# Expert weights as 2 MiB transfers into ten pair places, with the SBUF pools laid out anew

## The chip, the cores and the metric

The kernel is one program on 1 core of a Trainium2 chip. Its metric is the device time of one execution in microseconds (us), and the time of a kernel is the median of several executions. Beside the times there is one profiled execution with its trace: engines PE (TensorE), DVE (VectorE), ACT (ScalarE), POOL (GpSimd) and SP (SyncE, which here only issues transfers).

## What is computed

Two transformer blocks on 256 tokens of width 1024, all in float32. What matters here is how much weight each part reads:

```python
# first block: mixing (short convolution, gated delta rule, attention), then
u = causal_dwconv(h @ w_ffn_up[l], w_ffn_conv[l])
x = x + (jax.nn.silu(gate) * val) @ w_ffn_down[l]
# second block: modulation, two attentions, then 32 experts, four for each token
mod = jax.nn.silu(c) @ w_ada[l] + b_ada[l]
proj = h @ w_in[l]
...
hh = xb @ w1[e] + b1[e]
return swiglu_clamped(hh) @ w2[e] + b2[e]
```

Every expert has 8 MiB of `w1` and 4 MiB of `w2`, so 32 experts read 384 MiB. The dense weights of both blocks are 91 MiB.

## The kernel before

**Slabs.** All weights are packed on the host into slabs of 1 MiB: 128 partitions with 2048 float32 each, a row of 8 KB to a partition. `ws_in` holds the dense slabs in the order of their use, `we_in` twelve slabs for each expert (eight of `w1`, four of `w2`). One transfer on SP's queue brings one slab.

**Dense part.** A pool "A" of six places (`NA = 6`) takes the dense slabs. `load_slabs` (L192) issues the load of slab n once slab n-6 has been read in the program's order (L196), and `slab_read` (L251) calls it. There are two kinds of dense slab. The kind "s" is split by ACT and DVE or POOL into two float32r parts (`split`, L381; the hi part is L388, the lo part L393), two units to a slab, four units ahead of the products that use them. The kind "a" (`ada`, L475) is read by PE directly, at L483, and eight of them make one third of the modulation. The list `WS` mixes the two kinds: three "a" slabs ahead of the 15th "s" slab, five ahead of the 21st, one each ahead of the 39th, 42nd, 45th and 48th, and eight more inside the second block's attention. PE reads an "a" slab later than ACT and DVE split the "s" slabs behind it, since splitting runs ahead. Which of the six places a load gets is decided by the pool (L199): it takes one that has been given back.

**Expert part.** `load_m` (L215) loads the slabs of the experts in the order of `ORDER`. Places stand in the string `TURNS`, one letter for each of 19 slabs, named for the pool that holds it: X, A, B, C, D, E and O. They come free one after another as the dense part ends, and are then filled (`load_all`, L235). When PE has read a slab, `free_m` (L240) loads the next into the same place, but for the place "O", which is given back; so 18 places go round. `first_rounds` (L1693) and `second` (L1731, L1736) are the expert's products; an expert has a capacity of 32 to 128 tokens (`CAPS`), in pieces of 64 and 32, and its slabs are freed in its last piece.

**Queue.** All these transfers stand in SP's queue in the order of the program, and SP waits for one before it issues the next. A transfer also waits for the eighth before it, since eight semaphores go round.

```python
            if n >= NA and n - NA not in read:
                break
            if n < len(WS):
                t = slabs.tile([P, SW], F32, name="w")
```

Of the kernel before, what the change touches and what calls it, by code (L numbers as in the profile page):

```python
# [10 lines left out]
F32 = mybir.dt.float32  # L11
# [10 lines left out]
P = 128  # L22
T = 256
# [8 lines left out]
BIG = 3.0e38  # L32
NA = 6

TURNS = "XAAABBDODAAACCCCEEE"
NS = len(TURNS)
# [125 lines left out]
def kernel(ctx: ExitStack, tc: tile.TileContext, x_in, cols_in, rows_in, const_in, cona_in, conb_in, rpb_in,  # L162
# [4 lines left out]
    small = ctx.enter_context(tc.tile_pool(name="small", bufs=2))  # L167
    pools = {k: ctx.enter_context(tc.tile_pool(name="slabs" + k, bufs=TURNS.count(k))) for k in "ABCE"}
    slabs = pools["A"]
# [20 lines left out]
    read = set()  # L190

    def load_slabs(upto=10 ** 6):  # L192

        while state["loaded"] < min(upto, len(WS) + NA):
            n = state["loaded"]
            if n >= NA and n - NA not in read:  # L196
                break
            if n < len(WS):
                t = slabs.tile([P, SW], F32, name="w")  # L199
                for h in range(1 if n else 2):  # L200
                    o = slice(0, SW) if n else slice(h * UW, (h + 1) * UW)
                    nc.sync.dma_start(t[:, o], ws_in[n, :, o])
                s_slab[n] = t
            else:
                load_m([m for m in range(NS) if TURNS[m] == "A"][n - len(WS)])
            state["loaded"] += 1
# [8 lines left out]
    def load_m(m, pool=None):  # L215

        pos, i = divmod(m, 12)
        if pos >= len(ORDER):
            return
        rank = ORDER[pos]  # L220
        i = ((0, 2, 4, 6, 1, 3, 5, 7) if CAPS[rank] == 32 else (0, 2, 1, 3, 4, 6, 5, 7))[i] if i < 8 else i
# [142 lines left out]

    so = ctx.enter_context(ExitStack())


    with sx:
# [41 lines left out]

        hTh = pools["B"].tile([P, KC, T], F32R, name="hTh", tag="w")
        hTl = pools["B"].tile([P, KC, T], F32R, name="hTl", tag="w")
        yTh = pools["E"].tile([P, KC, T], F32R, name="yTh", tag="w")
        yTl = pools["E"].tile([P, KC, T], F32R, name="yTl", tag="w")
        xn = pools["E"].tile([P, 2, D], F32, name="xn", tag="w")

# [549 lines left out]
        with ExitStack() as s2:  # L966
# [40 lines left out]
            with ExitStack() as s3:  # L1007
# [77 lines left out]
                def add_norms(c):  # L1085
# [12 lines left out]
                    for h in range(2):  # L1098
# [9 lines left out]

            pools["X"] = ctx.enter_context(tc.tile_pool(name="slabsX", bufs=TURNS.count("X"), side="right",
                                                        reuse_waits="tile"))  # L1110
            s4 = sx.enter_context(ExitStack())
# [6 lines left out]
            load_all("X")  # L1118
            with ExitStack() as s3:
# [30 lines left out]
            with ExitStack() as s3:  # L1150
# [207 lines left out]
                def projections2():  # L1358
# [15 lines left out]
                    for kc in range(KC - LAST):  # L1374
                        while count["joined"] <= kc:
                            yield 0, 0.1
                        if "D" not in pools and (count["turned"] == 8 or kc == KC - LAST - 1):
                            while count["turned"] < 8:
                                yield 0, 0.1
                            s4.close()  # L1380
                            for n in "DO":
                                pools[n] = (ctx if n == "D" else so).enter_context(
                                    tc.tile_pool(name="slabs" + n, bufs=TURNS.count(n), side="right", reuse_waits="tile"))
                            load_all("DO")
# [109 lines left out]

    load_all("CE")
    s6 = ctx.enter_context(ExitStack())
# [185 lines left out]
    def first_rounds(w, blk, w1, onehot, free=None):  # L1682
# [33 lines left out]
    def second(w, blk, acts, w2, free=None):  # L1716
# [9 lines left out]
        for bi, bl in enumerate(BO):  # L1726
# [52 lines left out]
    def spare(name):  # L1779

        t = [m_pool[m] for m in range(12 * NE - NS + 1, 12 * NE - 12) if m_pool[m] in "BD"][len(spares)]
        spares.append(pools[t].tile([P, SW], F32, name=name, tag="w"))
        return spares[-1]
# [11 lines left out]
    for pos, rank in enumerate(ORDER):  # L1795
        m0_ = 12 * pos
        w1 = lambda bl, i: m_slab[m0_ + 2 * BO.index(bl) + i].rearrange("p (k n) -> p k n", k=4)
        free = lambda ks: free_m([m0_ + k for k in ks])
        w2 = lambda bi: m_slab[m0_ + 8 + bi].rearrange("p (k n) -> p k n", k=2)
        nxt = None  # L1800
# [32 lines left out]
        if pos == 0:  # L1833
            so.close()
            ek2 = ctx.enter_context(tc.tile_pool(name="ek2", bufs=2, side="right", reuse_waits="tile"))
            for _ in que:
# [28 lines left out]

    fs = [spare("fs") for _ in range(2)]
    fr = late.tile([P, 2], F32, name="fr")
# [41 lines left out]
    with tc.For_i(0, n_over, 1):  # L1909
        with ExitStack() as s7:  # L1910
# [6 lines left out]

            def load(i):
                t = slabs.tile([P, SW], F32, name="w")
                nc.sync.dma_start(t, we_in[ds(reg, 1), i].rearrange("a p n -> p (a n)"))  # L1920
                return t

            for n in range(4):
# [5 lines left out]
                def w1(bl, i):  # L1929
                    if (bl, i) not in w1t:  # L1930
                        w1t[bl, i] = load(2 * BO.index(bl) + i).rearrange("p (k n) -> p k n", k=4)
# [5 lines left out]
                w2t = [load(8 + i).rearrange("p (k n) -> p k n", k=2) for i in range(4)]  # L1937
                combine(blk, second(w, blk, a, lambda bi: w2t[bi]), into_acc)
# [33 lines left out]
def pack(inp):  # L1972
# [38 lines left out]
    w1, wd = f("w1_2")[0], f("w2_2")[0]  # L2011
    we = np.empty((NE, 12, P, SW), np.float32)
    a = w1.reshape(NE, KC, P, 4, 256, 2).transpose(0, 3, 2, 1, 5, 4)
    a = a.reshape(NE, 4, P, 2, 4 * 512).transpose(0, 1, 3, 2, 4)
    b = wd.reshape(NE, 4, 2, P, D).transpose(0, 1, 3, 2, 4).reshape(NE, 4, P, 2 * D)
    for i, bl in enumerate(BO):
        we[:, 2 * i:2 * i + 2] = a[:, bl]
        we[:, 8 + i] = b[:, bl]
    b1 = f("b1_2")[0].reshape(NE, 4, 256, 2).transpose(0, 1, 3, 2).reshape(NE, 2048)
# [47 lines left out]
```

## Time and profile before

| | us |
|---|---|
| median of 3 runs | 1521.78 (1520.45 to 1521.88) |
| the profiled execution, own time | 1518.86 |
| its span, first to last instruction | 1517.1 |
| PE busy | 1384.4 (91%) |
| DVE, ACT, POOL busy | 556.9, 449.1, 91.8 |

The profiled execution took 2.92 us less than the median. Up to about 555 us the program is the dense part, from 559 us to 1500 us the experts, and the last 17 us are the final norm and the output.

### The profile page before, as it was taken

To read this page: it belongs to the slowest core of one execution; us is meant where nothing else is said; L and a number is where in the kernel's file an instruction comes from. 1 tells how busy PE (TensorE), PEld (TensorE's weight loads), DVE (VectorE), ACT (ScalarE), POOL (GpSimd) and SP (SyncE) were. 2 spreads that over 40 slices of the span, in tenths; PEclk is the share of its full clock that TensorE was granted. 3 is DMA by queue.
4 is the path that set the end of the run, shared out by engine and by line. 5 is a ranking of instruction groups with operands and counts; after the bars stand their busy time and mean duration, and the time that the engine had idled before them with its cause. 6 is when DMAs were issued, how large, how long until landed. Compare 5 with 4: busy or idle time off the path is not lost.

```text
span 1517.1 us, 22468 instructions
## 1 busy us (share of the span) xinstructions
PE 1384.4 (91%) x8859; PEld 738.7 (49%) x8863; DVE 556.9 (37%) x1234; ACT 449.1 (30%) x975; POOL 91.8 (6%) x42
## 2 busy tenths in 40 slices
PE   6999979999999999999999999999999987988774
PEld 6898779998668753333333333333333322222111
DVE  4854687776767741222212122221121101111102
ACT  6554545555646641111111111111121101101111
POOL 3322150000310000000000000000000000000000
PEclk9999999999999999999999999999999999999887
DMA  7322575666666489999999999999999999999994
GB/s 309 123 101 85 223 278 212 263 220 227 203 255 245 167 359 357 419 421 421 377 421 386 388 414 416 421 421 420 420 421 421 420 421 420 421 421 420 421 421 183
DMA packets 71087, 506.72 MB, mean 334 GB/s; under 512 B 8096, under 2 KB 8352, under 8 KB 9952
## 3 DMA queue, kind: packets, MB, share of 16 engines
q1 hardware_dynamic: 70112, 503.50, 82.4%
q10 hardware_dynamic: 864, 1.72, 0.3%
q8 instruction: 72, 1.18, 0.3%
q14 instruction: 39, 0.32, 0.1%
HBM read 504.14 MB, written 1.05 MB: 333 GB/s over the span
## 4 chain that ended last, share of the span: by engine, by line
PE 61%; DMA 29%; DVE 5%; ACT 3%; issue 1%; SPq 0%; POOL 0%; ACTq 0%; DVEq 0%; POOLq 0%
DMA w<-in_we 28%; PE mm L1693 17%; PE mm L433 14%; PE mm L1736 6%; PE acc L1759 3%; PE acc L467 2%; PE acc L468 2%; PE acc L469 2%; PE mm L1651 2%; PE mm L1731 2%; DVE u L393 2%; DMA w<-in_ws 1%; PE mm L810 1%; PE mm L483 1%; PE mm L1662 1%
## 5 line engine op out<-in xcount | busy, mean ns | idle before, releaser
L1693 PE MATMUL mm<-w,xT 128*64 128x512 f32 (+1 forms) x2432 | 464.8, 633 | 56.8 <-DMA w<-in_we 56.5
L1693 PEld LDWEIGHTS mm<-w,xT 128*64 128x64 f32 (+1 forms) x2432 | 136.9, 130 | 366.8 <-issue 260.5
L1702 DVE TENSOR_SCALAR h<-mm 128x256 f32<-128x256 f32 x58 | 24.6, 425 | 728.2 <-PE mm L1698 728.2
L433 PE MATMUL mm<-hTh,u 128*128 128x256 f32 x1376 | 263.4, 289 | 8.8 <-DVE fcv L1043 7.2
L433 PEld LDWEIGHTS mm<-hTh,u 128*128 128x128 f32 x1376 | 220.4, 194 | 18.5 <-issue 14.3
L433 PE MATMUL mm<-hTl,u 128*128 128x256 f32 x688 | 196.3, 285 | 0.8 <-DVE hTl L422 0.8
L393 DVE TENSOR_TENSOR u<-w,u 128x1024 fp32r<-128x1024 f32 x115 | 160.8, 1403 | 68.0 <-ACT u L388 67.9
L1703 ACT ACTIVATE a<-h 128x256 f32<-128x256 f32 x58 | 24.2, 417 | 521.5 <-DVE h L1702 521.5
L388 ACT ACTIVATE u<-w 128x1024 fp32r<-128x1024 f32 x134 | 140.1, 1056 | 40.3 <-PE acc L469 30.0
L1736 PE MATMUL mm<-w,aT 128*64 128x512 f32 x640 | 141.7, 595 | 5.5 <-ACT aT L1714 5.4
L433 PEld LDWEIGHTS mm<-hTl,u 128*128 128x128 f32 x688 | 133.4, 194 | 2.0 <-DVE hTl L422 1.0
L1736 PEld LDWEIGHTS mm<-w,aT 128*64 128x64 f32 x640 | 44.1, 137 | 90.2 <-issue 79.1
L1741 ACT ACTIVATE y<-mm 128x512 f32<-128x512 f32 x38 | 22.7, 597 | 207.4 <-PE mm L1736 138.5
L1731 PE MATMUL mm<-w,aT 128*32 128x512 f32 x576 | 65.7, 595 | 9.9 <-ACT aT L1714 9.9
L1895 POOL TENSOR_TENSOR fs<-fs,x 128x512 f32<-128x512 f32 x1 | 1.3, 1261 | 960.6 <-ACT fr L300 960.6
L1651 PE MATMUL mm<-x,S 128*32 128x256 f32 (+1 forms) x448 | 56.7, 460 | 2.5 <-DVE S L1638 2.5
L393 POOL TENSOR_TENSOR u<-w,u 128x1024 fp32r<-128x1024 f32 x19 | 46.9, 2469 | 134.7 <-ACT u L388 134.7
L1043 DVE SCALAR_TENSOR_TENSOR fcv<-mm,cols,fcv 128x255 f32<-128x255 f32 x88 | 42.4, 482 | 26.6 <-ACT fcv L1040 25.1
L1669 ACT ACTIVATE xT<-mm,mod,gs 128x64 f32<-128x64 f32 (+1 forms) x152 | 46.6, 386 | 2.1 <-PE mm L1662 1.5
L1671 DVE TENSOR_SCALAR xT<-mm,gs,mod 128x64 f32<-128x64 f32 (+1 forms) x152 | 38.7, 320 | 3.0 <-PE mm L1662 3.0
L1731 PEld LDWEIGHTS mm<-w,aT 128*32 128x32 f32 x576 | 16.7, 109 | 46.8 <-issue 30.6
L1651 PEld LDWEIGHTS mm<-x,S 128*32 128x32 f32 (+1 forms) x448 | 18.6, 119 | 39.6 <-issue 28.3
(555 smaller groups left out, 1461.9 us busy)
## 6 DMA issues: line engine op xcount, KB each, us to landing
w<-in_we SPq DMA_DIRECT2D x384, 1024.0 KB, 19.8
w<-in_ws SPq DMA_DIRECT2D x90, 1024.0 KB, 5.0
nb<-in_rpb SPq DMA_DIRECT2D x4, 512.0 KB, 7.6
x<-in_x SPq DMA_DIRECT2D x2, 512.0 KB, 6.1
w<-in_ws SPq DMA_DIRECT2D x2, 512.0 KB, 7.6
bt<-in_b SPq DMA_DIRECT2D x3, 256.0 KB, 8.3
out<-fs SPq DMA_DIRECT2D x3, 256.0 KB, 3.1
grow<-in_wf ACTq DMA_DIRECT2D x1, 512.0 KB, 3.9
```

The costliest lines, as they stand in the source:

```text
L388: nc.scalar.activation(hi, raw, AF.Copy)
L393: eng.tensor_tensor(lo, raw, hi, op=OP.subtract)
L433: nc.tensor.matmul(b[:, 0:T], w[:, k, :], h[:, k, :], start=(n == 0), stop=(n == 3 * KC - 1))
L467: nc.tensor.matmul(o, th[:, kc, t], wh[:, w], start=first, stop=False)
L1043: nc.vector.scalar_tensor_tensor(t[:, sh:], b[:, :T - sh], w(2 - sh), t[:, sh:], op0=OP.mult, op1=OP.add)
L1651: nc.tensor.matmul(b[p * tb:(p + 1) * tb, 0:n], S[:, c, p * tb:(p + 1) * tb], x[:, c, p * n:(p + 1) * n], start=(c == 0), stop=(c == 1))
L1669: nc.scalar.activation(dst, src, AF.Identity, scale=gs[:, kc:kc + 1], bias=mod[:, 24 + kc:25 + kc])
L1671: nc.vector.tensor_scalar(dst, src, gs[:, kc:kc + 1], mod[:, 24 + kc:25 + kc], op0=OP.mult, op1=OP.add)
L1693: nc.tensor.matmul(b[p * tb:(p + 1) * tb, :], xT[:, k, q * tb:(q + 1) * tb], w1(p * nr + rd, kc // 4)[:, kc % 4, :], start=(kc == 0), stop ...
L1731: nc.tensor.matmul(b[p * tb:(p + 1) * tb, :], aT[:, 0, j, p0 * tb:(p0 + 1) * tb], w2(bi)[:, j, h * 512:(h + 1) * 512], start=(bi == 0), st ...
L1736: nc.tensor.matmul(b[p * tb:(p + 1) * tb, :], aT[:, rd, j, p0 * tb:(p0 + 1) * tb], w2(bi)[:, j, p * 512:(p + 1) * 512], start=(bi == 0 and ...
L1759: nc.tensor.matmul(acc[c][h], lhsT, rhs, start=False, stop=False, skip_group_check=True)
```

## The change

The experts' slabs are packed in pairs, two slabs side by side in one row: a transfer has 128 rows of 16 KB, 2 MiB. Ten places of 2 MiB stand in the new `TURNS`; all of them go round, so there are 20 MiB in place of 18 (19 at the start). The two slabs of a pair are those that are used together: two blocks of `w1` columns for the same half of the depth, or two neighbours of `w2`. A pair is freed when both are read.

The three pairs of pool A also take the dense slabs, slab by slab. They are no longer given out by the pool: slab n goes to half (n - N0) mod 6 of the three tiles `w_pair`, with N0 = len(WS) - 6 = 81. The rule for when a load is put into the program is the same as before. An expert's pair in A is loaded when both dense slabs of its halves are read.

The split parts `u` and the tile `xn` get pools of their own (`parts`, `xnp`), whose space the pools "C" and "G" take over after the dense part. `hTh` and `hTl` are halves of one tile, and so are `yTh` and `yTl`. The place "F" exists from the start.

```diff
-NA = 6
-TURNS = "XAAABBDODAAACCCCEEE"
+PW = 2 * SW
+NA = 3
+TURNS = "FABADACCEG"
...
+    w_pair = [slabs.tile([P, PW], F32, name="w") for _ in range(NA)]
+    N0 = len(WS) - 2 * NA
...
-            if n >= NA and n - NA not in read:
+            j = n - len(WS)
+            if n >= 2 * NA and not ({N0 + 2 * j, N0 + 2 * j + 1} if j >= 0 else {n - 2 * NA}) <= read:
                 break
-            if n < len(WS):
-                t = slabs.tile([P, SW], F32, name="w")
+            if j < 0:
+                i = (n - N0) % (2 * NA)
+                t = w_pair[i // 2][:, i % 2 * SW:(i % 2 + 1) * SW]
...
-        pos, i = divmod(m, 12)
+        pos, i = divmod(m, 6)
...
-        t = pools[m_pool[m]].tile([P, SW], F32, name="w")
+        t = pools[m_pool[m]].tile([P, PW], F32, name="w")
         nc.sync.dma_start(t, src)
...
         while state["freed"] in m_freed:
-            if m_pool[state["freed"]] != "O":
-                load_m(state["next"], m_pool[state["freed"]])
-                state["next"] += 1
+            load_m(state["next"], m_pool[state["freed"]])
+            state["next"] += 1
             state["freed"] += 1
...
-            t = pools["C"].tile([P, 2, UW], F32R, name="u", tag="w")
+            t = parts.tile([P, 2, UW], F32R, name="u")
...
-                    free([2 * BO.index(p * nr + rd) + kc // 4 for p in range(R)])
+                    free([j + kc // 4 for j in ((0, 2) if R == 4 else (2 * rd,))])
...
-            if free:
-                free([8 + bi])
+            if free and bi % 2:
+                free([4 + bi // 2])
```

**Order.** PE, DVE, ACT and POOL have the same compute instructions in the same order in both programs. What moves is on SP's queue. The first place is the end of the first block's mixing, where the first third of the modulation is computed. `w` are the tiles that a load fills, with the buffer's number; behind it stand the semaphores for which the load waits. Those named DMAHW are of earlier transfers, PE, DVE and Pool of the readers of what lay there. Before:

```order
L202 DMA w_1729<-in_ws 128x2048 [waits DMAHW1_49,DVE_49,Pool_49]
L202 DMA w_1735<-in_ws 128x2048 [waits DMAHW6_49,PE_49]
L202 DMA w_1924<-in_ws 128x2048 [waits DMAHW7_49,PE_49]
L202 DMA w_1926<-in_ws 128x2048 [waits DMAHW2_49,DMAHW0_49,DVE_49]
L202 DMA w_1928<-in_ws 128x2048 [waits DMAHW3_49,DVE_49]
L202 DMA w_1930<-in_ws 128x2048 [waits DMAHW4_49,DVE_49]
L202 DMA w_1932<-in_ws 128x2048 [waits PE_49]
L202 DMA w_1978<-in_ws 128x2048 [waits DMAHW0_49,PE_49]
```

The same eight slabs after the change, w_95 to w_97 being the three pairs:

```order
L211 DMA w_97<-in_ws 128x2048 [waits DMAHW6_49,PE_49]
L211 DMA w_95<-in_ws 128x2048 [waits DMAHW7_49,PE_49]
L211 DMA w_95<-in_ws 128x2048 [waits DMAHW0_49,PE_49]
L211 DMA w_96<-in_ws 128x2048 [waits DMAHW1_49,DVE_49,Pool_49]
L211 DMA w_96<-in_ws 128x2048 [waits DMAHW2_49,DVE_49]
L211 DMA w_97<-in_ws 128x2048 [waits DMAHW3_49,DVE_49]
L211 DMA w_97<-in_ws 128x2048 [waits DMAHW4_49,DVE_49]
L211 DMA w_95<-in_ws 128x2048 [waits DMAHW5_49,Pool_49]
```

They are the slabs 20 to 27 of `WS` (counted from 0). Before, the first three waits were for a split and two "a" slabs, and the third "a" slab came up at the seventh; now the three "a" slabs (14, 15 and 16) are waited for by the first three loads, and the other five stand behind them.

The second place is the first block's feed-forward, at the 39th "s" slab. Before:

```order
L202 DMA w_3412<-in_ws 128x2048 [waits DMAHW6_49,DMAHW4_49,DVE_49]
L202 DMA w_3414<-in_ws 128x2048 [waits DMAHW7_49,DMAHW5_49,DVE_49]
L202 DMA w_3416<-in_ws 128x2048 [waits DMAHW0_49,DVE_49]
L202 DMA w_3418<-in_ws 128x2048 [waits DMAHW3_49,DVE_49]
L202 DMA w_3594<-in_ws 128x2048 [waits PE_49]
```

And after the change:

```order
L211 DMA w_95<-in_ws 128x2048 [waits DMAHW4_49,PE_49]
L211 DMA w_96<-in_ws 128x2048 [waits DMAHW6_49,DMAHW5_49,DVE_49]
L211 DMA w_96<-in_ws 128x2048 [waits DMAHW7_49,DVE_49]
L211 DMA w_97<-in_ws 128x2048 [waits DMAHW0_49,DVE_49]
L211 DMA w_97<-in_ws 128x2048 [waits DMAHW2_49,PE_49]
```

The wait for PE's reading of the "a" slab stood at the fifth of these loads and stands at the first now; the same comes again at the next two "a" slabs.

## Rows read from the trace of the kernel before

**Rows 1.** The page's second part: 40 equal slices of the span, transfers.

```profile
DMA  7322575666666489999999999999999999999994
GB/s 309 123 101 85 223 278 212 263 220 227 203 255 245 167 359 357 419 421 421 377 421 386 388 414 416 421 421 420 420 421 421 420 421 420 421 421 420 421 421 183
```

**Rows 2.** The page's fourth part: shares of the chain that ended last.

```profile
PE 61%; DMA 29%; DVE 5%; ACT 3%; issue 1%; SPq 0%; POOL 0%; ACTq 0%; DVEq 0%; POOLq 0%
```

**Rows 3.** Windows of the experts: busy PE, PEld, DVE, ACT, POOL; PE clock, DMA share, GB/s.

```profile
600.00:720.00 120.00, 115.78 (x634) 41.17 (x632) 28.14 (x96) 19.50 (x53) 0.00 (x0) 1.00 1.01 420
...
830.00:850.00 20.00, 19.61 (x130) 6.58 (x128) 1.18 (x3) 3.17 (x8) 0.00 (x0) 1.00 0.78 298
...
950.00:1495.00 545.00, 474.66 (x2758) 152.80 (x2756) 90.73 (x290) 77.35 (x211) 0.00 (x0) 0.95 1.01 419
```

**Rows 4.** The chain in order of time, at 1045 us (start, us, what).

```profile
1045.55 19.76 DMA w<-in_we
```

**Rows 5.** Windows of the start: 4 KB rows alone, then 8 KB rows alone.

```profile
9.70:11.00 1.30, 1.30 (x7) 1.30 (x8) 0.62 (x6) 0.68 (x4) 0.00 (x0) 1.00 1.01 413
12.20:13.50 1.30, 1.30 (x7) 1.08 (x6) 1.30 (x6) 1.30 (x4) 0.00 (x0) 1.00 1.03 429
```

**Rows 6.** SP's timeline: two issues of expert slabs around 835 us.

```profile
834.62 0.33 SPq L231 DMA_DIRECT2D w<-in_we  x1
836.34 0.33 SPq L231 DMA_DIRECT2D w<-in_we  x1
```

**Rows 7.** The page's sixth part: dense loads, KB of one, median us to landing.

```profile
w<-in_ws SPq DMA_DIRECT2D x90, 1024.0 KB, 5.0
```

**Rows 8.** SP's timeline, the dense slabs 22, 23, 26 and 28.

```profile
160.34 0.33 SPq L202 DMA_DIRECT2D w<-in_ws  x1
167.28 0.33 SPq L202 DMA_DIRECT2D w<-in_ws  x1
184.20 0.33 SPq L202 DMA_DIRECT2D w<-in_ws  x1
186.94 0.40 SPq L202 DMA_DIRECT2D w<-in_ws  x1
```

**Rows 9.** PE's timeline from 182 us (start, us, instruction, count).

```profile
183.08 3.64 PE L483 MATMUL mm<-w,silc 128*32 128x512 f32 x32
186.65 1.09 PE L339 MATMUL mm<-cst,xn 128*128 128x128 f32 x8
```

**Rows 10.** ACT's and DVE's timelines from 187 us.

```profile
187.34 2.17 ACT L420 ACTIVATE hTh<-mm,cols 128x128 fp32r<-128x128 f32 x8
189.35 3.00 ACT L388 ACTIVATE u<-w 128x1024 fp32r<-128x1024 f32 x3
198.91 1.06 ACT L388 ACTIVATE u<-w 128x1024 fp32r<-128x1024 f32 x1 [5.22 <-DMA w<-in_ws]
191.44 3.72 DVE L393 TENSOR_TENSOR u<-w,u 128x1024 fp32r<-128x1024 f32 x2 [0.76 <-ACT u L388]
```

**Rows 11.** A window while the transfers of `bt` (32 partitions) run.

```profile
191.00:193.00 2.00, 2.00 (x19) 2.00 (x18) 1.56 (x1) 1.35 (x2) 1.93 (x1) 1.00 1.08 238
```

**Rows 12.** The feed-forward: issue of the slab of the 43rd "s", its split, PE, and the chain.

```profile
314.19 0.33 SPq L202 DMA_DIRECT2D w<-in_ws  x1
330.91 1.06 ACT L388 ACTIVATE u<-w 128x1024 fp32r<-128x1024 f32 x1 [0.32 <-PE acc L469]
333.61 1.06 PE L483 MATMUL mm<-w,silc 128*32 128x512 f32 x8
334.68 11.71 PE mm L433 x96
```

**Rows 13.** DVE's and PE's timelines in the second block's attention.

```profile
426.91 1.21 DVE L393 TENSOR_TENSOR u<-w,u 128x1024 fp32r<-128x1024 f32 x1
432.89 1.06 PE L483 MATMUL acc<-w,silc 128*32 128x512 f32 x8
```

**Rows 14.** Waits between 400 and 480 us (waiter, releaser, us, times, longest).

```profile
ACT u L388 <- DMA w<-in_ws: 3.8, 2, 2.0
```

More of the change, by code (lines that the diff above doesn't have):

```diff
@@ L167 @@
     small = ctx.enter_context(tc.tile_pool(name="small", bufs=2))
-    pools = {k: ctx.enter_context(tc.tile_pool(name="slabs" + k, bufs=TURNS.count(k))) for k in "ABCE"}
+    pools = {k: ctx.enter_context(tc.tile_pool(name="slabs" + k, bufs=TURNS.count(k))) for k in "ABEF"}
     slabs = pools["A"]
@@ L178 @@
     sx = ctx.enter_context(ExitStack())
+    parts = sx.enter_context(tc.tile_pool(name="parts", bufs=4))
+    xnp = sx.enter_context(tc.tile_pool(name="xnp", bufs=1))
     hp = sx.enter_context(tc.tile_pool(name="hp", bufs=1))
@@ L204, in load_slabs @@
             else:
-                load_m([m for m in range(NS) if TURNS[m] == "A"][n - len(WS)])
+                load_m([m for m in range(NS) if TURNS[m] == "A"][j])
             state["loaded"] += 1
@@ L409, in split_ahead @@
                 state["split"] += 1
[L411 to L415, printed above, removed]
+        hT2 = pools["B"].tile([P, 2, KC, T], F32R, name="hT2", tag="w")
+        yT2 = pools["E"].tile([P, 2, KC, T], F32R, name="yT2", tag="w")
+        hTh, hTl, yTh, yTl = hT2[:, 0], hT2[:, 1], yT2[:, 0], yT2[:, 1]
+        xn = xnp.tile([P, 2, D], F32, name="xn")
         def take_scaled(scale):
@@ L1106 @@
                 last_products(4, lambda i, cs, wh, wl: down(NFF - 4 + i, cs, wh, wl), add_norms, False)
-            pools["X"] = ctx.enter_context(tc.tile_pool(name="slabsX", bufs=TURNS.count("X"), side="right",
-                                                        reuse_waits="tile"))
             s4 = sx.enter_context(ExitStack())
@@ L1380, in projections2 @@
                             s4.close()
[L1381 to L1384, printed above, removed]
+                            pools["D"] = ctx.enter_context(tc.tile_pool(name="slabsD", bufs=1, side="right",
+                                                                        reuse_waits="tile"))
+                            load_all("D")
                         wh, wl = unit()
@@ L1467 @@
             keep_warm(WARM[5])
+    for k in "CG":
+        pools[k] = ctx.enter_context(tc.tile_pool(name="slabs" + k, bufs=TURNS.count(k), reuse_waits="tile"))
+    ek2 = ctx.enter_context(tc.tile_pool(name="ek2", bufs=2, side="right", reuse_waits="tile"))
     psa = ctx.enter_context(tc.tile_pool(name="psm", bufs=1, space=PSUM, reuse_waits="tile"))
@@ L1493, in open_work @@
         return w
-    load_all("CE")
+    load_all("CEG")
     s6 = ctx.enter_context(ExitStack())
@@ L1779, in spare @@
     def spare(name):
-        t = [m_pool[m] for m in range(12 * NE - NS + 1, 12 * NE - 12) if m_pool[m] in "BD"][len(spares)]
-        spares.append(pools[t].tile([P, SW], F32, name=name, tag="w"))
+        t = [m_pool[m] for m in range(6 * NE - NS, 6 * NE - 6) if m_pool[m] in "BD"][len(spares)]
+        spares.append(pools[t].tile([P, PW], F32, name=name, tag="w"))
         return spares[-1]
@@ L1795 @@
     for pos, rank in enumerate(ORDER):
-        m0_ = 12 * pos
-        w1 = lambda bl, i: m_slab[m0_ + 2 * BO.index(bl) + i].rearrange("p (k n) -> p k n", k=4)
+        m0_ = 6 * pos
+        of_pair = lambda j, i: m_slab[m0_ + j][:, i * SW:(i + 1) * SW]
+        w1 = lambda bl, i: of_pair(BO.index(bl) // 2 * 2 + i, BO.index(bl) % 2).rearrange("p (k n) -> p k n", k=4)
         free = lambda ks: free_m([m0_ + k for k in ks])
-        w2 = lambda bi: m_slab[m0_ + 8 + bi].rearrange("p (k n) -> p k n", k=2)
+        w2 = lambda bi: of_pair(4 + bi // 2, bi % 2).rearrange("p (k n) -> p k n", k=2)
         nxt = None
@@ L1833 @@
         if pos == 0:
-            so.close()
-            ek2 = ctx.enter_context(tc.tile_pool(name="ek2", bufs=2, side="right", reuse_waits="tile"))
             for _ in que:
@@ L1864 @@
     s6.close()
-    fs = [spare("fs") for _ in range(2)]
+    fs_ = spare("fs")
+    fs = [fs_[:, c * D:(c + 1) * D] for c in range(2)]
     fr = late.tile([P, 2], F32, name="fr")
@@ L1916, with load @@
                 nc.vector.tensor_scalar(oc[:, i:i + 1], ocap[:, 0:1], 64.0 * i, None, op0=OP.add)
-            def load(i):
+            def load(j, i):
                 t = slabs.tile([P, SW], F32, name="w")
-                nc.sync.dma_start(t, we_in[ds(reg, 1), i].rearrange("a p n -> p (a n)"))
+                nc.sync.dma_start(t, we_in[ds(reg, 1), j, :, i * SW:(i + 1) * SW].rearrange("a p n -> p (a n)"))
                 return t
@@ L1930, in w1 @@
                     if (bl, i) not in w1t:
-                        w1t[bl, i] = load(2 * BO.index(bl) + i).rearrange("p (k n) -> p k n", k=4)
+                        n_ = BO.index(bl)
+                        w1t[bl, i] = load(n_ // 2 * 2 + i, n_ % 2).rearrange("p (k n) -> p k n", k=4)
                     return w1t[bl, i]
@@ L1936 @@
                     pass
-                w2t = [load(8 + i).rearrange("p (k n) -> p k n", k=2) for i in range(4)]
+                w2t = [load(4 + i // 2, i % 2).rearrange("p (k n) -> p k n", k=2) for i in range(4)]
                 combine(blk, second(w, blk, a, lambda bi: w2t[bi]), into_acc)
@@ L2016, in pack @@
     for i, bl in enumerate(BO):
-        we[:, 2 * i:2 * i + 2] = a[:, bl]
-        we[:, 8 + i] = b[:, bl]
+        for h in range(2):
+            we[:, i // 2 * 2 + h, :, i % 2] = a[:, bl, h]
+        we[:, 4 + i // 2, :, i % 2] = b[:, bl]
+    we = we.reshape(NE, 6, P, PW)
     b1 = f("b1_2")[0].reshape(NE, 4, 256, 2).transpose(0, 1, 3, 2).reshape(NE, 2048)
```

14 lines of the change are left out of this document (6 added, 8 removed).

## The prediction

> **What bounds the kernel now.** I read the slices first. From 606 us on, the transfers move 419 to 421 GB/s in nearly every slice, with dips to 377 and 386; before, in the dense part, they move 85 to 359 [rows 1]. So bytes can bound the experts, not the dense part. The shares of the chain say the same in another way: PE 61%, DMA 29% [rows 2]. The windows tell where the bound changes: between 600 and 720 us PE is busy in 115.78 of 120 us while the transfers already run at full share; between 830 and 850 us the transfers' share falls to 0.78, because places are not free; from 950 to 1495 us PE is busy in 474.66 of 545 us and the transfers move 419 GB/s without a hole [rows 3]. The chain's DMA piece at 1045 us gives the price of a MiB: eight transfers are in flight together, and 19.76 us [rows 4] are eight of them, 2.47 us each (2.49 at 421 GB/s).
>
> From this two things follow. What the experts' transfers gain after the last wait for a place, at about 850 us, is gained at the end. And what the dense part loses is lost at the end too, unless the transfers can run on meanwhile; they can't, since the places are full when PE is late.
>
> **What doesn't change.** The arithmetic on PE, DVE, ACT and POOL, in order and size; the bytes (384 MiB for the experts); the issues on SP, 0.33 us each [rows 6], which have 2.5 us apiece: 192 fewer cost and give nothing.
>
> **Gain 1: one more pair goes round.** 18 MiB go round now, 20 then, so the transfers may be 2 MiB further ahead of PE at the last wait for a place: 2 × 2.49 = 5.0 us. But a pair is free only when both slabs are read, and the two places at 835 us came free at 834.62 and 836.34 [rows 6], 1.72 us apart: 5.0 - 1.7 = **-3.3 us**. Bounds: 0 (PE, not places, sets the pace up to 850 us) and -5.0 (nothing lost by pairs).
>
> **Gain 2: rows of 16 KB.** 4 KB rows ran at 413 GB/s, 8 KB rows at 429 in a short window [rows 5] and at 421 in the long run [rows 1]; 16 KB rows are not in this trace. As a time for each row on one of 16 engines: 4096 B / (413/16) = 158.7 ns, 8192 B / (421/16) = 311.3 ns, so 8 KB take 6.1 ns less than two of 4 KB; a fixed cost of that size saves 3.05 ns on each 8 KB when rows double, 1.0%. The upper bound is the best rate seen, 429 against 421, 1.9%. I take 1.4%, between the two; over the 650 us from 845 to 1495 us that is **-9 us**. Bounds: 0 (long rows are no quicker) and -12.4 (1.9%). [...]
>
> **Loss A: the end of the mixing.** By the listing of the order, slab 22 now takes the half of slab 16, the third "a" slab, and waits for PE's reading of it, with the "a" slabs 23 to 26 behind it on SP's queue. These were issued at 167.28 (slab 23) up to 184.20 (slab 26), and slab 22 at 160.34 [rows 8]. PE reads "a" slabs in one run of 32 matmuls from 183.08, 3.64 us for four slabs [rows 9]; the first of the four is slab 16, read at 183.08 + 0.91 = 184.0. So all five loads are issued from about 184.1. One alone lands after 5.0 us [rows 7], at 189.1; the next follow by 2.49: slabs 23, 24, 25 at 191.6, 194.1 and 196.6. PE wanted the last of these by 185.8 and was done with it at 186.7; now it is done at 196.6 + 0.91 = 197.5, 10.8 us late. Behind it on PE stands L339 at 186.65, and from its output L420 on ACT at 187.34, three splits L388 at 189.35, and DVE's L393 that ended at 191.44 + 3.72 = 195.16 [rows 9, 10]: all by 10.8 later, so 205.9. Slab 28 takes the half of slab 22 and is now issued only after that split, at 205.9 instead of 186.94 [rows 8]. It lands 5.0 us later at the earliest, 210.9; with slab 27 and the 32-partition transfers of `bt`, which run at 238 GB/s under full share [rows 11], ahead of it, at up to 214.5. ACT began its split at 198.91, after 5.22 us of waiting for that very load [rows 10]. So the feed-forward starts 12.0 to 15.6 us late; I take **+15 us**, nearer the upper end since `bt` does lie in between. Bounds: 12 and 17. What gives nothing back: the feed-forward that follows is a chain of PE.
>
> **Loss B: three "a" slabs in the feed-forward.** The load of the slab of the 43rd "s" was issued at 314.19; now it is the first to wait for PE's reading of an "a" slab, which ends at 333.61 + 1.06 = 334.7 [rows 12]. It lands 5.0 later, 339.7; its splits (1.06 on ACT as at 330.91 [rows 12], and about as long for the lo part) are ready at 341.8 to 342. PE's chain piece from 334.68 lasts 11.71 us for four projections, 2.93 each [rows 12]; the third begins at 334.68 + 5.86 = 340.5. That is 1.5 us late, three times over: **+5 us**, bounds 3 and 7.
>
> **Loss C: the attention stage.** Eight more "a" slabs stand there, and a load behind them that waited for a split waits for PE's reading now: the split ended at 426.91 + 1.21 = 428.1, PE's reading at 432.89 + 1.06 = 433.95 [rows 13], 5.8 us later. ACT's splits there already waited 3.8 us in two waits for loads [rows 14], so a later issue can be felt. Bounds: 0 (the loads ahead cover it) and 6 (all of it is felt, once); I take **+3 us**, the middle, since no row shows how far these loads run ahead. The first expert pair now goes out ahead of dense loads there, one transfer of 5 us in a stage with loads ahead: nothing, at most 1.
>
> **The sum.** 15 + 5 + 3 - 3.3 - 9 = +10.7 us. The profiled execution took 1518.86, so 1529.6 of the same kind; the median is 2.92 above it, so **1532.5**. All bounds together give -2.4 to +30.
>
> **Rivals.**
> *Long rows give nothing.* The rows of 4 and 8 KB differ by 2 to 4% at most, and the fixed cost may lie in something that doesn't shrink again. Then only Gain 1 is left: 23 - 3.3 = +19.7, **1541.5**. For it: the share of the engines stands at 1.01 already [rows 3], so the wire is full; against it: the two rates in rows 5 do differ.
> *The dense delay is absorbed* (the other side). If the end hung on bytes alone, the transfers would run on while the dense part is late, and only the gains would be left: -12.3, **1509.5**. This decides by whether the transfers ever wait for places after 600 us. Against it: the share of 0.78 between 830 and 850 us [rows 3] and the dips to 377 and 386 [rows 1], where they did wait for PE; a shift of PE shifts these waits. For it: the dips are short, and PE is at full share there only in part.
> *The change doesn't do what it says*: a half of a pair is waited for as a whole tile. The listing speaks against it, as every half has a wait of its own; I give it part of the last case.
> *More than 30 us lost in the dense part*, as one late load makes the next one late: from +18, about 1545 to 1555.
>
> **How the numbers follow.** About 0.2%, 3.0 us, is what a measurement of this kernel can tell from no change. Forecast 0.68, long rows nothing 0.17, dense delay absorbed 0.10, more lost 0.05. The forecast's own lower end (row gain at its bound and dense losses at theirs) touches no change: I give 0.06 of its chance to "same", and a little of the absorbed case also (half of the gain): 0.07 same; faster 0.10; slower 0.83. The range leaves out the absorbed case and the worst one: 1521 (nearly the lower bounds together) to 1546 (long rows nothing, with the dense losses somewhat above my values).
>
> **What would show it.** PE should wait for dense loads at L483 between 185 and 198 us, and ACT at L388 should wait to about 211 to 214 us (Loss A); L433 should wait for splits near 340 us and at two more places (Loss B). The experts' first products should come 20 to 25 us later. From 950 us on the rate should read 424 to 429 GB/s, and eight transfers in flight, 16 MiB then, should take about 39.0 us in the chain (2 × 19.76 less 1.4%); 421 GB/s would mean that long rows give nothing. The dip of the transfers around 835 us should be there still, some 20 us later. The forecast is wrong if L483 doesn't wait there, or if the rate exceeds 430.

## The result, and the profile after

The changed kernel takes 1534.41 us (median of 4 runs, 1532.92 to 1535.05) where the kernel before, run on the same chip, takes 1521.12: a ratio of 1.0092, 95% interval [1.0077, 1.0108], or 13.3 us more. The forecast was 1532.5 us, 10.7 us more. The profiled execution took 1534.30 us (before: 1518.86), its span is 1532.5.

The slices of the changed kernel, to be read beside [rows 1]:

```profile
DMA  7322385635668469999899899999999999999993
GB/s 306 121 101 84 124 304 184 260 152 209 267 194 319 156 243 407 417 428 426 377 394 416 348 428 415 428 427 427 427 428 426 427 427 428 428 427 427 428 428 163
```

Two things stand in them. The long run of the experts reads 427 and 428 GB/s where it read 420 and 421. And the fifth slice, from 153 to 192 us, reads 124 where it read 223: there the transfers did not go out. The shares of the chain that ended last moved with both:

```profile
PE 67%; DMA 21%; DVE 5%; ACT 4%; issue 1%; SPq 0%; POOL 0%; ACTq 0%; DVEq 0%; POOLq 0%
```

DMA's share fell from 29% [rows 2] to 21%. In the chain in order of time the unbroken pieces of eight expert transfers, 16 MiB now, begin at 1226 us and not at 1045 as in [rows 4]; start and length in us:

```profile
1226.62 38.82 DMA w<-in_we
1265.55 39.04 DMA w<-in_we
...
1462.92 38.99 DMA w<-in_we
```

So the bytes got cheaper (about 39.0 us for 16 MiB against 2 × 19.76), and with that PE set the pace for longer before the bytes did. The windows, with the columns of [rows 3], show the wait in the dense part, the last large wait for places, and the run that follows:

```profile
180.00:200.00 20.00, 10.88 (x66) 4.91 (x68) 6.32 (x22) 5.87 (x20) 2.34 (x1) 0.83 0.65 263
860.00:880.00 20.00, 19.61 (x129) 6.90 (x130) 3.35 (x12) 3.73 (x11) 0.00 (x0) 1.00 0.76 302
950.00:1495.00 545.00, 474.55 (x2901) 153.52 (x2896) 94.06 (x304) 79.69 (x219) 0.00 (x0) 0.96 1.01 427
```

PE is busy in 10.88 of the 20 us from 180 us. The transfers' share falls to 0.76 at 860 to 880 us; it was 0.78 at 830 to 850 [rows 3]. Here is the cause of the first window, in the order in which it happens. SP's timeline (start, us, instruction, count), to be read beside [rows 8]:

```profile
160.32 0.33 SPq L211 DMA_DIRECT2D w<-in_ws  x1
...
185.04 2.51 SPq L211 DMA_DIRECT2D w<-in_ws  x5
204.95 1.54 SPq L1018 DMA_DIRECT2D bt<-in_b  x3
206.79 0.35 SPq L211 DMA_DIRECT2D w<-in_ws  x1
```

Between 161.5 and 185 us SP issues nothing. Then five loads go out at once, the slabs 22 to 26; slab 28 follows at 206.79. PE's timeline, beside [rows 9] (L488 is L483 of before):

```profile
183.91 1.06 PE L488 MATMUL mm<-w,silc 128*32 128x512 f32 x8
192.29 1.94 PE L488 MATMUL mm<-w,silc 128*32 128x512 f32 x8 [7.31 <-DMA w<-in_ws]
194.78 1.61 PE L488 MATMUL mm<-w,silc 128*32 128x512 f32 x8 [0.56 <-DMA w<-in_ws]
197.26 1.06 PE L488 MATMUL mm<-w,silc 128*32 128x512 f32 x8 [0.86 <-DMA w<-in_ws]
```

The first eight matmuls read slab 16 and free its half. The next eight wait 7.31 us for the first "a" slab, and the two groups behind them go at the pace of the transfers, 2.5 us apart. Two of the groups also take longer, 1.94 and 1.61 us instead of 1.06. The window of the first of them, which came after those 7.31 us of idle time, shows a granted clock of 0.50 (the column after POOL; 0.64 over the second, 1.00 over the third group, of 1.06 us):

```profile
192.00:194.30 2.30, 1.94 (x8) 0.20 (x8) 0.00 (x0) 0.00 (x0) 0.00 (x0) 0.50 1.03 435
```

This cost nothing here, since the group behind each of the two still waited for its transfer (0.56 and 0.86 us). ACT's timeline, beside [rows 10] (L425 is L420 of before, L394 is L388):

```profile
198.95 2.17 ACT L425 ACTIVATE hT<-mm,cols 128x128 fp32r<-128x128 f32 x8 [10.69 <-PE mm L347]
...
215.72 1.06 ACT L394 ACTIVATE u<-w 128x1024 fp32r<-128x1024 f32 x1 [11.35 <-DMA w<-in_ws]
```

L425 starts 11.6 us after its start before (187.34), and the split of slab 28 16.8 us after (198.91). Behind that split, DVE's lo part of it takes 1.2 us longer than before, beside an operation of POOL on `bt`. DVE's timelines, before and after:

```profile
200.00 4.38 DVE L393 TENSOR_TENSOR u<-w,u 128x1024 fp32r<-128x1024 f32 x1 [3.94 <-ACT u L388]
```

```profile
216.81 5.60 DVE L399 TENSOR_TENSOR u<-w,u 128x1024 fp32r<-128x1024 f32 x1 [9.14 <-ACT u L394]
```

How the delay grows and shrinks can be read from starts of one and the same ACT instruction in both kernels. Of the kernel before: in the first group of the feed-forward, at its end, at the end of the attention, at the first expert, at an expert in the middle, at the last:

```profile
206.44 0.42 ACT L1052 ACTIVATE gh<-fcv 128x256 fp32r<-128x256 f32 x1 [2.60 <-DVE fcv L1049]
...
389.89 0.60 ACT L1091 ACTIVATE mm<-xn 128x512 f32<-128x512 f32 x1 [3.37 <-DVE xn L1090]
...
516.59 0.38 ACT L472 ACTIVATE yTh<-mm 128x256 fp32r<-128x256 f32 x1 [1.18 <-PE mm L1297]
...
566.88 0.42 ACT L1703 ACTIVATE a<-h 128x256 f32<-128x256 f32 x1 [5.36 <-DVE h L1702]
...
1150.96 0.42 ACT L1703 ACTIVATE a<-h 128x256 f32<-128x256 f32 x1 [6.94 <-DVE h L1702]
...
1493.20 0.42 ACT L1703 ACTIVATE a<-h 128x256 f32<-128x256 f32 x1 [17.36 <-DVE h L1702]
```

The same six of the changed kernel:

```profile
224.48 0.42 ACT L1057 ACTIVATE gh<-fcv 128x256 fp32r<-128x256 f32 x1 [3.81 <-DVE fcv L1054]
...
412.11 0.60 ACT L1096 ACTIVATE mm<-xn 128x512 f32<-128x512 f32 x1 [2.67 <-DVE xn L1095]
...
544.44 0.38 ACT L477 ACTIVATE yT<-mm 128x256 fp32r<-128x256 f32 x1 [2.56 <-PE mm L1300]
...
594.72 0.42 ACT L1708 ACTIVATE a<-h 128x256 f32<-128x256 f32 x1 [5.36 <-DVE h L1707]
...
1178.76 0.42 ACT L1708 ACTIVATE a<-h 128x256 f32<-128x256 f32 x1 [6.94 <-DVE h L1707]
...
1508.63 0.42 ACT L1708 ACTIVATE a<-h 128x256 f32<-128x256 f32 x1 [17.12 <-DVE h L1707]
```

The differences, beside the sums of the prediction's terms up to that point:

| up to | late, us | this stretch adds | forecast |
|---|---|---|---|
| start of the feed-forward | 18.04 | 18.0 (Loss A) | 15 |
| its end | 22.22 | 4.2 (Loss B) | 5 |
| end of the attention | 27.85 | 5.6 (Loss C) | 3 |
| first expert | 27.84 | 0.0 | 0 |
| expert in the middle | 27.80 | 0.0 | 0 |
| last expert | 15.43 | -12.4 (both gains) | -12.3 |

From the first expert to 1151 us of the kernel before, the delay stays the same: there PE sets the pace of both kernels, and cheaper bytes help neither. Both gains come after that. Loss B can be seen at three waits of ACT for loads in the feed-forward, where the kernel before has none; the first of them (the others come at 377.49 and 397.09 us):

```profile
357.76 2.00 ACT L394 ACTIVATE u<-w 128x1024 fp32r<-128x1024 f32 x2 [8.96 <-DMA w<-in_ws]
```

### The profile page after: what moved, and what is told of

Same layout as the page of the kernel before. It is cut to its first block, busy times and chain, and to the rows that moved or that the text cites. A ratio compares the mean times of both kernels' runs of the same rounds, so it can differ in the third digit from the quotient of the medians.

```text
span 1532.5 us, 21741 instructions
## 1 busy us (share of the span) xinstructions
PE 1377.1 (90%) x8859; PEld 737.4 (48%) x8863; DVE 553.4 (36%) x1234; ACT 449.0 (29%) x975; POOL 91.8 (6%) x42
## 4 chain that ended last, share of the span: by engine, by line
PE 67%; DMA 21%; DVE 5%; ACT 4%; issue 1%; SPq 0%; POOL 0%; ACTq 0%; DVEq 0%; POOLq 0%
PE mm L1698 21%; DMA w<-in_we 18%; PE mm L438 13%; PE mm L1741 8%; PE acc L1764 3%; DMA w<-in_ws 3%; PE mm L1656 3%; PE mm L1736 3%; PE acc L472 3%; PE acc L473 3%; PE acc L474 3%; DVE u L399 2%; PE mm L815 1%; ACT u L394 1%; ACT aT L1719 1%
## 5 line engine op out<-in xcount | busy, mean ns | idle before, releaser
L1698 PE MATMUL mm<-w,xT 128*64 128x512 f32 (+1 forms) x2432 | 446.4, 632 | 61.3 <-DMA w<-in_we 60.7
L1698 PEld LDWEIGHTS mm<-w,xT 128*64 128x64 f32 (+1 forms) x2432 | 130.8, 130 | 360.1 <-issue 274.8
L438 PE MATMUL mm<-hT,u 128*128 128x256 f32 x2064 | 270.4, 291 | 13.5 <-DVE fcv L1048 9.2
L438 PEld LDWEIGHTS mm<-hT,u 128*128 128x128 f32 x2064 | 259.5, 197 | 27.2 <-issue 18.5
L394 ACT ACTIVATE u<-w 128x1024 fp32r<-128x1024 f32 x134 | 139.7, 1056 | 64.2 <-DMA w<-in_ws 42.4
L1048 DVE SCALAR_TENSOR_TENSOR fcv<-mm,cols,fcv 128x255 f32<-128x255 f32 x88 | 42.3, 481 | 15.9 <-ACT fcv L1045 14.3
L472 PE MATMUL acc<-u,gh 128*128 128x512 f32 x88 | 34.9, 397 | 0.0
L473 PE MATMUL acc<-u,gh 128*128 128x512 f32 x88 | 34.9, 397 | 0.0
```

What stands on the lines that cost most here:

```text
L438: nc.tensor.matmul(b[:, 0:T], w[:, k, :], h[:, k, :], start=(n == 0), stop=(n == 3 * KC - 1))
L472: nc.tensor.matmul(o, th[:, kc, t], wh[:, w], start=first, stop=False)
L473: nc.tensor.matmul(o, th[:, kc, t], wl[:, w], start=False, stop=False)
L1698: nc.tensor.matmul(b[p * tb:(p + 1) * tb, :], xT[:, k, q * tb:(q + 1) * tb], w1(p * nr + rd, kc // 4)[:, kc % 4, :], start=(kc == 0), stop ...
```

## The experiments

All the runs below are compared with the kernel before on the same chip; it stood between 1519.3 and 1521.0 us.

**1. The halves as they come free** (`e1_halves`). A table `HALF` of 87 numbers replaces the fixed turn; it gives slab n the half that was read first, so every dense load waits for the same reader as in the kernel before. The pairs, the long rows and the ten places stay.

```diff
-                i = (n - N0) % (2 * NA)
+                i = HALF[n]
```

> The changed kernel, but each dense slab takes the half that was read first (a table of 87 halves), as the pool of the kernel before gave them out; the last six slabs still lie in pairs. Theory 'late halves' (the 26 us by which the experts start later come from loads that wait for PE's reading of an "a" slab): the experts start within 1 us of the kernel before, both gains stay, 1534.4 - 26 = 1508 us, ratio to the kernel before about 0.992. Rival 'end by bytes' (an earlier start of the experts is lost again, as the transfers set the end): between 1519 and 1530. Rival 'the new layout itself delays the dense part' (tiles, pair transfers beside dense loads): still near 1534.

Measured: 1510.19 us, ratio 0.9929 [0.9913, 0.9946]. The main theory holds: without the late halves the same change is faster than the kernel before, and an earlier start of the experts is kept to the end. But the first expert starts 5.4 us late (572.33 against 566.88) where "within 1 us" was expected. The delay is 1.7 us at the end of the feed-forward and 5.4 us at the end of the attention: 3.7 us of Loss C are there although no load waits for another reader than before.

**2. The same up to slab 33 only** (`e2_first`), from there on with a period of six:

```diff
+HALF = [0, 1, 3, 5, 4, 2, 0, 1, 3, 5, 4, 2, 0, 1, 3, 5, 4, 2, 0, 1, 2, 3, 5, 0, 1, 2, 4, 0, 1,
+        2, 3, 4, 5, 0, 1, 2, 3, 4, 5, 0, 1, 2, 3, 4, 5, 0, 1, 2, 3, 4, 5, 0, 1, 2, 3, 4, 5, 0,
...
-                i = (n - N0) % (2 * NA)
+                i = HALF[n]
```

> As the run before it, but halves by first reading only up to slab 33, fixed with a period of six after that: it undoes the wait at the end of the mixing (Loss A) and keeps the later ones. If the three losses stand beside each other: 1534.4 - 18 = 1516.5 us, the experts 8 to 9 us later than in the kernel before. Rival: the waits in the feed-forward and the attention (Losses B and C) come only because the loads are late already from A: then they go too, 1508 us.

Measured: 1515.41 us, ratio 0.9972 [0.9960, 0.9983]. Against the changed kernel that is 0.0120 of the time, 18 us, which is Loss A alone. Loss B stays: between the start and the end of the feed-forward this run loses 4.3 us to the kernel before, the first run 0.3 us. So A and B add up, and both come from the halves. Its first expert is 12.2 us late, where 8 to 9 were expected: the attention stage loses 6.7 us in this run, more than the 5.6 of the changed kernel.

**3. Nine places** (`e3_nine`), on the first run; a spare tile at the very end may then lie in a place of A too.

```diff
-TURNS = "FABADACCEG"
+TURNS = "FABADACEG"
...
-        t = [m_pool[m] for m in range(6 * NE - NS, 6 * NE - 6) if m_pool[m] in "BD"][len(spares)]
+        t = [m_pool[m] for m in range(6 * NE - NS, 6 * NE - 6) if m_pool[m] in "ABD"][len(spares)]
```

> The first of these runs with nine pair places in place of ten (one of pool C's two left out), 18 MiB go round as in the kernel before. Theory 'lead' (2 MiB more ahead at the last wait for a place): 3 us slower than with ten places (2 to 5 us). Rival 'places don't count': within 1 us of it.

Measured: 1514.50 us, ratio 0.9958 [0.9941, 0.9974], 4.3 us more than with ten places: the lead counts, at the upper part of what was expected. Both runs free their places in pairs, so this is the price of the lead alone.

**4 to 6. What makes the bytes cheaper.** The change doubles the row and the transfer together. Three runs take them apart: two transfers of 1 MiB with 8 KB rows (`e4_cols`), two transfers of 1 MiB with 16 KB rows (`e5_parts`), one transfer of 2 MiB with 8 KB rows (`e6_rows`, for which the two slabs lie one behind the other in HBM).

```diff
-        nc.sync.dma_start(t, src)
+        for h in range(2):
+            nc.sync.dma_start(t[:, h * SW:(h + 1) * SW], src[:, h * SW:(h + 1) * SW])
```

> The changed kernel, but each expert pair comes in two transfers of 1 MiB, one for each slab: rows of 8 KB, 8 MiB in flight. Theory 'row size': the rate after 1045 us falls from 427 to 421 GB/s, about 1.5% of some 600 us: 1542 to 1544 us. Theory 'bytes in flight' (16 MiB in flight keep the engines fuller): the same here. If neither, 1534.

```diff
-        nc.sync.dma_start(t, src)
+        for h in range(2):
+            nc.sync.dma_start(t[h * 64:(h + 1) * 64, :], src[h * 64:(h + 1) * 64, :])
```

> The changed kernel, but each expert pair comes in two transfers of 1 MiB by halves of the partitions: 64 rows of 16 KB, 8 MiB in flight. Theory 'row size': 427 GB/s stay, 1534 us. Theory 'bytes in flight': 421 GB/s, 1542 to 1544 us.

```diff
-            src = we_in[rank, i]
+            src = we_in[rank, i].rearrange("a p n -> p a n")
...
-        nc.sync.dma_start(t, src)
+        nc.sync.dma_start(t.rearrange("p (a n) -> p a n", a=2), src)
...
-    we = np.empty((NE, 6, P, 2, SW), np.float32)
+    we = np.empty((NE, 6, 2, P, SW), np.float32)
```

> The changed kernel, but the two slabs of a pair lie one behind the other in HBM: one transfer of 2 MiB with 256 rows of 8 KB, 16 MiB in flight. Theory 'row size': 421 GB/s, 1542 to 1544 us. Theory 'bytes in flight': 427 GB/s stay, 1534 us.

Measured: 1540.94 us (1.0139 [1.0122, 1.0156]) and 1541.83 us (1.0146 [1.0129, 1.0163]) with the 8 KB rows, in 1 MiB and in 2 MiB transfers. Both read 421 GB/s; here is the window of the one with 2 MiB:

```profile
1045.00:1490.00 445.00, 376.77 (x2260) 121.11 (x2256) 75.55 (x245) 62.28 (x174) 0.00 (x0) 0.93 1.01 421
```

So 16 MiB in flight don't help: the row does. From the ratios, going back to 8 KB rows costs 0.0047 to 0.0054 of the time, 7 to 8 us. The third run, with 64 neighbouring partitions to a transfer, told nothing of that question: it took 2204.89 us (2075.09 to 2284.18). Its window:

```profile
700.00:1000.00 300.00, 188.96 (x798) 62.17 (x800) 33.71 (x115) 25.49 (x69) 0.00 (x0) 0.78 1.01 216
1400.00:1900.00 500.00, 328.78 (x1596) 103.99 (x1590) 52.34 (x171) 44.43 (x123) 0.00 (x0) 0.81 1.01 254
```

The transfers' share is full (1.01), at little more than half the rate. In HBM such a transfer reads 1 MiB in one piece, as in the kernel before (421 GB/s), so the reading side does not explain it.

**7. The missing cell** (`e9_alternate`): 1 MiB transfers with 16 KB rows again, but to the even and to the odd partitions.

```diff
-        nc.sync.dma_start(t, src)
+        for h in range(2):
+            nc.sync.dma_start(t[h::2, :], src[h::2, :])
```

> The changed kernel, but each expert pair comes in two transfers of 1 MiB, one for the even and one for the odd partitions: 64 rows of 16 KB each. It tells why the transfers by halves of the partitions ran at 216 GB/s. Theory 'few partitions at a time' (64 rows are too few for the 16 engines): about 216 GB/s again, 2150 to 2250 us. Theory 'neighbouring partitions share a way in' (the half of the partitions that lie together is served by half the ways): 427 GB/s and 1534 us if row size alone counts for the rest, 421 GB/s and 1542 us if the MiB in flight do.

Measured: 1532.70 us, 1.0076 [1.0059, 1.0093], no slower than the changed kernel. The window:

```profile
1045.00:1490.00 445.00, 378.81 (x2287) 126.73 (x2280) 76.24 (x246) 63.36 (x176) 0.00 (x0) 0.94 1.01 427
```

With 8 MiB in flight and 16 KB rows the rate is 427. That settles it: the row size gives the rate (427 and 421 GB/s), and which partitions a transfer touches can nearly halve it (216 to 254 GB/s).

**8 and 9. A first guess at Loss C, which fell.** The 2 MiB of the first expert pair (place F) go out just ahead of the load of `cb`, which POOL needs. Two runs move that pair behind the attention, with the halves as they come free (`e7_late`) and with the fixed halves (`e8_after_late`).

```diff
-            load_all("F")
...
-                            load_all("D")
+                            load_all("FD")
```

> The run with the halves as they come free, and the load of the first expert pair (place F) moved from ahead of the second block's attention to where the pair of place D is loaded, some 90 us later. Theory 'F ahead of cb' (in the attention stage 4 to 5 us are lost although every dense load waits as in the kernel before; the 2 MiB of F go out just ahead of the load of cb, which takes 12.4 us instead of 7.9, so POOL's addition into nb starts 5 us later and lies over other splits on DVE): the 4 to 5 us go, 1505 to 1506 us. Rival: they have another cause in the new layout, 1510 us; or the pair is then missing at the experts' start, above 1511.

> The changed kernel with only that one load moved, the halves fixed as in the change. Theory 'F ahead of cb' is all of Loss C: 1534.4 - 5 = 1529.5 us. Rival (the halves' waits are Loss C, as the prediction put it): 1534 us.

Measured: 1513.00 us (0.9947 [0.9930, 0.9964]) and 1535.75 us (1.0107 [1.0086, 1.0127]): neither got faster, and the first lost 3 us (its first expert is 8.1 us late, where it was 5.4). What did change is the time at which POOL starts, and what stands still meanwhile. POOL's and DVE's timelines of the first of the two:

```profile
411.40 9.03 POOL L1168 TENSOR_TENSOR nb<-nb,cb 128x2048 f32<-128x2048 f32 x2
```

```profile
411.44 4.58 DVE L1174 SCALAR_TENSOR_TENSOR lamt<-rows 128x64 f32<-128x64 f32 x1
...
416.30 4.14 DVE L1178 SCALAR_TENSOR_TENSOR lam<-lam 128x1 f32<-128x1 f32 x1 [0.27 <-ACT lam L1177]
```

An operation on a 128x1 tile takes 4.14 us (0.16 in the kernel before). In the kernel before and in the changed one it is the splits that are stretched, and at other times. DVE's timelines, of before (three splits), then of the changed kernel (single ones), whose POOL additions run from 438.88 to 449.70 us:

```profile
411.79 12.23 DVE L393 TENSOR_TENSOR u<-w,u 128x1024 fp32r<-128x1024 f32 x3 [0.69 <-ACT u L388]
```

```profile
438.56 1.22 DVE L399 TENSOR_TENSOR u<-w,u 128x1024 fp32r<-128x1024 f32 x1
442.39 2.95 DVE L399 TENSOR_TENSOR u<-w,u 128x1024 fp32r<-128x1024 f32 x1 [2.62 <-ACT u L394]
445.27 0.68 DVE L1199 COPY vd<-acc 128x512 f32<-128x512 f32 x1
445.87 4.92 DVE L399 TENSOR_TENSOR u<-w,u 128x1024 fp32r<-128x1024 f32 x1
```

In the first of the two runs POOL's first addition ends at 415.94 us and the operation that DVE started beside it at 416.02, the second addition at 420.43 and the 128x1 operation at 420.44.

**10 to 12. The same additions on DVE.** The second guess: POOL's two additions into `nb` hold DVE, and the new layout only moves them to where DVE's delay is on the path. They start 22.3 us after the end of the feed-forward in the kernel before, 25.8 in the first run and 26.8 in the changed kernel. Their result is first read some 65 us later. Three runs take them off POOL: the halves as they come free (`e10_halves_dve`), the changed kernel (`e11_after_dve`), the kernel before (`e12_before_dve`).

```diff
-                for c in range(2):
-                    vw = nb[:, c].rearrange("p r h c -> p (r h) c")
-                    nc.gpsimd.tensor_tensor(vw, vw, conb("win")[:, None, :].to_broadcast([P, 32, 64]), op=OP.add)
...
                         if i < 4:
+                            vw = nb[:, i // 2].rearrange("p r h c -> p (r h) c")[:, i % 2 * 16:i % 2 * 16 + 16]
+                            nc.vector.tensor_tensor(vw, vw, conb("win")[:, None, :].to_broadcast([P, 16, 64]),
+                                                    op=OP.add)
```

> The run with the halves as they come free, with POOL's two additions of the window mask into nb (some 5 us each) done by DVE instead, in four pieces of 128x1024 (about 1.2 us each) behind the keys of the first four heads. Theory 'POOL holds DVE' (while POOL adds into nb, DVE's operations come to a stop, two splits took 10.5 us instead of 2.4; the new layout only shifts this stop to where DVE's delay is on the path): Loss C goes and a part of what the stop costs in the kernel before also, 1510 less 4 to 9: 1501 to 1506 us. Rival (Loss C has another cause): 1510 us or above.

> The changed kernel with that one edit alone, the halves fixed. Theory 'POOL holds DVE': 1534.4 less 4 to 9: 1525 to 1530 us, and from the end of the feed-forward to the experts no more is lost against the kernel before with the same edit than 1 us. Rival (the wait of these loads for PE is Loss C, as the prediction put it): 1534 us, or 3 us and more lost there against the kernel before with the same edit.

> The kernel before with that one edit alone. Theory 'POOL holds DVE': its own stop lies where it costs little to 5 us: 1516 to 1521 us. The difference to the run with the halves as they come free and the same edit is then the two gains alone, 12 to 15 us.

Measured: 1501.93 us (0.9876 [0.9855, 0.9897]), 1527.09 us (1.0044 [1.0031, 1.0057]) and 1516.57 us (0.9969 [0.9957, 0.9980]), all three times within what was expected. The three splits that took 12.23 us in the kernel before take, with the edit:

```profile
412.62 3.50 DVE L393 TENSOR_TENSOR u<-w,u 128x1024 fp32r<-128x1024 f32 x3 [0.69 <-ACT u L388]
```

Most of Loss C is gone, but not all of it. Here are the end of the feed-forward and the end of the attention with the edit, in the kernel before and in the changed one:

```profile
390.73 0.60 ACT L1091 ACTIVATE mm<-xn 128x512 f32<-128x512 f32 x1 [3.37 <-DVE xn L1090]
...
513.74 0.38 ACT L472 ACTIVATE yTh<-mm 128x256 fp32r<-128x256 f32 x1 [2.47 <-PE mm L1293]
```

```profile
412.34 0.60 ACT L1096 ACTIVATE mm<-xn 128x512 f32<-128x512 f32 x1 [2.66 <-DVE xn L1095]
...
537.19 0.38 ACT L477 ACTIVATE yT<-mm 128x256 fp32r<-128x256 f32 x1 [2.24 <-PE mm L1296]
```

The changed kernel is 21.6 us late at the first point and 23.4 at the second (23.7 at the first expert). So 2.1 us are added between the feed-forward and the experts, where the theory had at most 1 and its rival 3 or more. The time between the two points, in all six kernels:

| us | additions on POOL | on DVE |
|---|---|---|
| kernel before | 126.70 | 123.01 |
| new layout, halves as they come free | 130.43 | 123.08 |
| new layout, halves fixed (the change) | 132.33 | 124.85 |

Without POOL's additions the new layout costs 0.1 us, and the fixed halves 1.8 more; with them it costs 3.7, and the fixed halves 1.9 more. So the two causes add up to Loss C: 3.7 from POOL's additions, which cost 7.4 us in the new layout against 3.7 in the kernel before, and 1.8 to 1.9 from loads that wait for PE. ACT's waits for loads in this stage say the same: 7.3 us with the halves fixed, 3.5 to 4.1 in the other four. Why the additions cost twice as much when they start 3.5 to 4.5 us later is argued, not shown: DVE is held for less time in the changed kernel (5.4 us in two splits) than before (8.7 us in three), so it must count which of its operations are held.

The first of the three beats both kernels: it is 1.2% faster than the kernel before, and takes 14.6 us less than that kernel with the same edit, which are put down to the two gains. Counted from the first expert, this pair of runs gains 15.9 us where the changed kernel gained 12.4 on the kernel before; what makes the difference is open.

## Why the prediction was right, point by point

- **Loss A**, forecast +15 with bounds 12 and 17, measured 18.0 at the start of the feed-forward, 18 us by the second run. The mechanism came step by step as written: five loads at 185.04 (forecast 184.1), PE's groups at 192.29, 194.78 and 197.26 (loads forecast to land at 191.6, 194.1 and 196.6), the issue of slab 28 at 206.79 (205.9), its split at 215.72 (211 to 214.5). The size was 3 us short, and 1 us past the upper bound. 0.9 us are the later issue of slab 28, nearly all of it from ahead of the place (PE reached slab 16 at 183.91, not at 183.08); 0.9 us are its landing (8.9 us from issue to split, 8.0 in the +15); 1.2 us are DVE's lo part of that split, held beside POOL (5.60 instead of 4.38), a term that the sum did not have. Tenths count little here: the same point lies at 206.44 and at 207.25 us in two runs whose programs are alike up to it.
- **Loss B**, forecast +5, measured 4.2, or 1.4 us on the mean for each of the three "a" slabs (forecast 1.5). The second run shows it apart from A.
- **Loss C**, forecast +3, measured 5.6, of which the forecast's own cause is a third. "A later issue can be felt" held: it costs 1.8 to 1.9 us, less than the 3 that were taken. The other 3.7 us stand in no term of the sum. The sentence that cost the first expert pair at "nothing, at most 1" looked at the dense loads alone. That pair also holds up the load of `cb` (12.4 us to landing instead of 7.9, and 4.2 to 5.4 with the pair moved away), and with it the start of POOL's additions, which hold DVE. Moving the pair away did not help, since the additions then began earlier still and held other operations of DVE.
- **Gain 1**, forecast -3.3 with bounds 0 and -5.0: 5.0 for the lead, less 1.7 for the freeing in pairs. Nine places instead of ten cost 4.3 us, which is the lead. What the freeing in pairs costs no run shows. The last large wait for places stood there again, some 30 us later.
- **Gain 2**, forecast -9 from a rate 1.4% higher: the rate rose from 421 to 427 GB/s, 1.4%, and 8 KB rows cost 7 to 8 us. The stretch over which it pays is shorter than the 650 us of the sum: places still ran out at 860 to 880 us, and a little in the slice from 920 to 958 us (415 GB/s). From 958 to the last expert at 1508 us, 550 us at 1.4% are 7.7 us. That the rate came out to the tenth of a per cent is luck: its bounds rest on windows of 1.3 us, and the 429 of its upper bound is not the best rate of the kernel before, where windows of 1 to 2 us between 10 and 16 us read from 410 to 463.
- **The rivals.** "Long rows give nothing" would have had 421 GB/s and 1541.5 us; the two runs with 8 KB rows stand at 1540.94 and 1541.83. "The dense delay is absorbed" fell: the last expert still ends 15.4 us late, and the first run, with A and B gone, keeps the earlier start to the end. In "More than 30 us lost" the sum is off: +18 on the median is about 1540, not 1545.

By the table the terms were off by +3.0, -0.8 and +2.6, the gains together by -0.1: +4.7 in all, on the profiled executions (15.4 us between them, as at the last expert). The dense part alone lost 27.8 us where 23 were forecast, so the sign "the experts' first products 20 to 25 us later" was missed. Between the medians the miss is 2.6 us, since the profiled execution of before lay 2.3 us under the median taken beside the changed kernel's. So the mechanism was right for A, B and the gains, but that the forecast of 1532.5 us came within 2 us of 1534.41 is in part luck.

## What to carry to other kernels

When a load gets a fixed place, ask who reads that place last in time, not in the program: a slab that PE reads late holds back every load that stands behind it on the queue, and 18 us came from one such slab. Which place a load gets costs no bytes, so a table that is written down once can give the places out in the order in which they are read. And where a change moves the start of an operation on POOL, look at what DVE does at that time, before putting the whole of a loss down to transfers.

## What the hardware showed that was not expected

- Expert transfers to 64 neighbouring partitions ran at 216 to 254 GB/s with the transfers' share at 1.01, to every second partition at 427. No run here shows why.
- While POOL adds 128x2048 elements, a DVE operation on a 128x1 tile took 4.14 us, and three splits took 12.23 instead of 3.50 us. There DVE was held until POOL was done, rather than slowed throughout: the 128x1 operation, 0.16 us long in the kernel before, ends at 420.44 us, POOL's two additions at 420.43. A copy out of PSUM (445.27 us in the changed kernel) took 0.68 us beside POOL, as it does with POOL idle (434.46 us in `e7_late`).
- Rows of 16 KB move 1.4% more than rows of 8 KB (427 against 421 GB/s), whether 8 or 16 MiB are in flight.
